# Keeping the split output weights in DRAM, moving the norm's squares to ScalarE, and a longer tile ring

## The chip, the cores and the metric

The kernel runs on one core of one Trainium2 chip, in one launch. The number that counts is the device time of that launch in microseconds (us). A core has five engines that run their own instruction streams: TensorE (PE, matrix products), VectorE (DVE), ScalarE (ACT), GpSimd (POOL) and SyncE (SP). They meet through semaphores. Data moves between DRAM and the on-chip SBUF by DMA; here SP starts nearly all DMAs and ACT a few. Products are accumulated in the eight banks of PSUM.

## The reference

Two layers on a sequence of 1024 tokens of 1024 channels. Layer 0 mixes tokens with RWKV-7, layer 1 with sparse attention (DSA). A convolutional gated FFN stands behind each. After each of the four blocks the residual is normalised:

```python
for i in range(DEPTH):
    if i % N_MIXERS == 0:
        h, v_first = rwkv7_time_mix(x, ...)      # ends with  return y @ w_o
    else:
        h = dsa_attention(x, ...)                # ends with  return o @ w_o
    x = layer_norm(DN_ALPHA * x + h, ln_g[i, 0], ln_b[i, 0])
    f = conv_ffn(x, ffn_w_up[i], ...)
    x = layer_norm(DN_ALPHA * x + f, ln_g[i, 1], ln_b[i, 1])
```

Everything is float32. The change touches `y @ w_o` and `o @ w_o` (each 1024x1024 times 1024x1024), the normalisation behind them, and the buffers of the RWKV block.

## The kernel before, in words

**Phases.** By the trace, RWKV runs to about 900 us with its output projection at 803 to 988 us, FFN 0 from about 1000 to 1740 us, DSA from 1740 to 2391 us with its output projection at 2157 to 2204 us (first half) and 2324 to 2391 us (second half), FFN 1 from about 2405 us to the end. Each block works on two halves of 512 tokens, so there are a first and a second half of each output projection.

**Split products.** A float32 product is made as three passes in a faster format. Each operand is split into `hi` (a cast, on ACT, line 54) and `lo = raw - hi` (on DVE or POOL, line 60); `mm3` (lines 65 to 67) then multiplies hi·hi, hi·lo and lo·hi. `wsplit` loads a 128x512 piece of a weight from DRAM by SP (line 124) into `wr` and splits it into `wh` and `wl`. Which engine makes `lo` stands in the table `CFG` ('p' POOL, 'v' DVE).

**Output projection.** `out_proj` handles the first half: for both column halves `ch` and eight row blocks `kt` it splits one weight piece and multiplies it with four token tiles; 16 pieces in all. `out_proj_last` handles the second half in stages. Its first stage uses pieces (kt 0 to 3, ch 0) and splits a set of "late" pieces ahead into storage that has come free (8 of them in RWKV, 12 in DSA); the next stage uses (kt 0 to 3, ch 1); its last four stages go token tile by token tile over the late pieces, add the residual and normalise. It loads and splits the weights again: 20 pieces in RWKV, where four are made twice, and 16 in DSA.

**Norm.** `residual` adds ALPHA times the input (line 143, DVE). `layer_norm_rows` takes mean and variance either by `bn_stats` and `bn_aggr` on DVE (lines 91 to 95), which the output projections use, or from sums that were collected before and two squares on ACT (lines 97 to 102), which the FFNs use already. Behind both come a power on POOL (`lnrs`, line 103), a small DVE step (`lnnm`, line 104), then the scaling (lines 106 to 111) on DVE, ACT and POOL.

**Rings.** In RWKV all 128x512 column tiles (`wh`, `wl`, `xmh`, `xml`, `xr`, `xm`) come from one ring of `k.NU` = 13 buffers, handed out in order; raw weights have their own ring `raw` of 3. In DSA's first half `wr`, `wl` and `wh` come in turn from a ring of six. A tile can be filled only when the last reader of the one that had its buffer is done. RWKV writes split pairs that it needs again to DRAM (`kept_w`, `kept_xm`) and reads them back later. The low-rank stage (`lora1`, `la` products, and `l2` products behind it) uses the four PSUM banks of `acc`.

**Order.** A scheduler lays the instructions of each engine into one fixed order ahead of time, by the order of the code and a priority; at run time each engine takes its stream in order, and a waiting instruction holds all behind it. That goes for SP's DMA queue as well.

Of the kernel before, what the change touches and what calls it, by code (L numbers as in the profile page):

```python
# [7 lines left out]
F32 = mybir.dt.float32  # L8
F32R = mybir.dt.float32r
BF16 = mybir.dt.bfloat16  # L10
AF = mybir.ActivationFunctionType
ALU = mybir.AluOpType
# [6 lines left out]
ALPHA = 4.0 ** 0.25  # L19
# [26 lines left out]
def f32(ap):  # L46
    return ap.bitcast(F32)


def split(k, raw, hi, lo, hi_eng="a", lo_eng="p"):  # L50

    nc = k.nc
    if hi_eng == "a":
        nc.scalar.copy(hi, raw)  # L54
    elif hi_eng == "v":
        nc.vector.tensor_copy(hi, raw)
    else:
        nc.gpsimd.tensor_scalar(hi, raw, 1.0, 0.0, ALU.mult, ALU.add)
    eng = nc.vector if lo_eng == "v" else nc.gpsimd
    eng.tensor_tensor(lo, raw, f32(hi), ALU.subtract)  # L60


def mm3(k, ps, lhs, rhs, start, stop, **kw):
    mm = k.nc.tensor.matmul
    mm(ps, lhs[0], rhs[0], start=start, stop=False, **kw)  # L65
    mm(ps, lhs[0], rhs[1], start=False, stop=False, **kw)  # L66
    mm(ps, lhs[1], rhs[0], start=False, stop=stop, **kw)  # L67
# [52 lines left out]
def wsplit(k, u, ap, n=512, lo_eng="v", raw=None):  # L120

    raw = (raw or u)("wr")[:, :n]
    lo, hi = u("wl", F32R)[:, :n], u("wh", F32R)[:, :n]
    k.nc.sync.dma_start(raw, ap)
    split(k, raw, hi, lo, "a", lo_eng)
    return hi, lo
# [10 lines left out]
    return Z  # L137


def residual(k, r, src, row, ch, ps):  # L140

    k.nc.sync.dma_start(r, src[row : row + 128, ch * 512 : (ch + 1) * 512])
    k.nc.vector.scalar_tensor_tensor(r, r, ALPHA, ps, ALU.mult, ALU.add)


def norm_store(k, pool, r, lnw, dst, row, eng="pp", **kw):
    layer_norm_rows(k, pool, r, *lnw, r, eng, **kw)
    for ch in range(2):
        k.nc.sync.dma_start(dst[row : row + 128, ch * 512 : (ch + 1) * 512], r[ch])


def out_proj(k, pool, u, raw, acc, res_tile, Z, w_ap, src, dst, hf, lnw):


    res = {}
    for ch in range(2):
        a = [acc("wo") for _ in range(4)]
        for kt in range(KT):
            w = wsplit(k, u, w_ap[kt * 128 : (kt + 1) * 128, ch * 512 : (ch + 1) * 512], lo_eng=CFG[("d" if raw is None else "") + "wo0"][kt], raw=raw)
            for tt in range(4):  # L160
                Zk = Z[kt // 4][:, :, kt % 4, tt * 128 : tt * 128 + 128]
                mm3(k, a[tt], (Zk[:, 0], Zk[:, 1]), w, kt == 0, kt == KT - 1)
            yield
        for tt in range(4):
            if ch == 0:
                res[tt] = res_tile()
            residual(k, res[tt][ch], src, (hf * 4 + tt) * 128, ch, a[tt])
    yield
    lnw = lnw()
    for tt in range(4):  # L170
        norm_store(k, pool, res[tt], lnw, dst, (hf * 4 + tt) * 128, CFG["ln1" if raw is None else "ln0"])
        yield


def out_proj_last(k, pool, u, raw, acc, acc1, wlate, nlate, res_tile, Z, w_ap, src, dst, hf, lnw):


    a = {}

    def w_of(kt, ch, u, lo_eng):  # L180
        return wsplit(k, u, w_ap[kt * 128 : (kt + 1) * 128, ch * 512 : (ch + 1) * 512], lo_eng=lo_eng, raw=raw)

    def part(tt, ch, kt, w):
        Zk = Z[kt // 4][:, :, kt % 4, tt * 128 : tt * 128 + 128]
        mm3(k, a[tt, ch], (Zk[:, 0], Zk[:, 1]), w, kt == 0, kt == KT - 1)

    late, order = {}, [(kt, 1) for kt in range(4)] + [(kt, ch) for ch in range(2) for kt in range(4, KT)]
    order = order[12 - nlate :]
    for tt in range(4):
        a[tt, 0] = acc("wo")  # L190
    for kt in range(4):
        w = w_of(kt, 0, u, CFG[("d" if raw is None else "") + "wl"][kt])
        for tt in range(4):
            part(tt, 0, kt, w)
        for kc in order[nlate // 4 * kt : nlate // 4 * (kt + 1)]:
            late[kc] = w_of(*kc, wlate, CFG[("d" if raw is None else "") + "wl2"])
    yield
    for pair in ((0, 1), (2, 3)):
        for tt in pair:
            a[tt, 1] = acc1("wo")  # L200
        for kt in range(4):
            w = late[kt, 1] if nlate == 12 else w_of(kt, 1, u, CFG[("d" if raw is None else "") + "wl3"][kt % 2])
            for tt in pair:
                part(tt, 1, kt, w)
        yield
    lnw = lnw()
    for tt in range(4):
        r = res_tile()
        for ch in range(2):
            for kt in range(4, KT):  # L210
                part(tt, ch, kt, late[kt, ch])
            residual(k, r[ch], src, (hf * 4 + tt) * 128, ch, a[tt, ch])
        norm_store(k, pool, r, lnw, dst, (hf * 4 + tt) * 128, CFG["ln3" if raw is None else "ln2"][2 * tt : 2 * tt + 2])
        yield


# [90 lines left out]
def rwkv(k, src, dst):  # L307
    nc, tc = k.nc, k.tc
# [8 lines left out]
    def u(name, dt=F32):  # L317
        return P_.tile([128, 512], dt, name=name, tag="u", bufs=k.NU)

    def t(name, dt=F32):  # L320
        return M_.tile([128, 512], dt, name=name, tag="t", bufs=5)
# [4 lines left out]
    def acc(name):  # L326
        return PS.tile([128, 512], F32, name=name, tag="acc", bufs=4)
# [70 lines left out]
    def raw(name):  # L398
        return P_.tile([128, 512], F32, name=name, tag="raw", bufs=3)

    def lora1(hf):
        xT = st[hf]["xT"]
        a = [acc("la") for _ in range(4)]
        for kt in range(KT):
            xx = t("xx")
            nc.vector.tensor_tensor(xx, xT[:, kt, 0:512], xT[:, kt, 1:513], ALU.subtract)
            w = raw("wl1")[:, :288]
            nc.sync.dma_start(w, k.w_l1[kt * 128 : (kt + 1) * 128, :])
            xm = {}
            for n in (3, 4, 5):  # L410
                xm[n] = u("xm")
                c = V_MIX + 8 * n + kt
                nc.vector.scalar_tensor_tensor(
                    xm[n], xx, k.vec[:, c : c + 1], xT[:, kt, 1:513], ALU.mult, ALU.add
                )

            for b, n, c0, c1, p0 in ((0, 3, 0, 64, 0), (1, 4, 64, 128, 64), (2, 5, 128, 256, 0), (3, 5, 256, 288, 96)):
                nc.tensor.matmul(
                    a[b][p0 : p0 + c1 - c0], w[:, c0:c1], xm[n], start=kt == 0, stop=kt == KT - 1
                )  # L420
        h = M_.tile([128, 512], F32, name="h", tag="h", bufs=1)
        nc.scalar.activation(h[:64], a[0][:64], AF.Tanh)
        nc.scalar.copy(h[64:], a[1][64:])
        tg = t("tg")
        nc.scalar.activation(tg, a[2], AF.Sigmoid)
        nc.sync.dma_start(gsc[hf, 0:128], tg)
        tg2 = t("tg2")
        nc.scalar.activation(tg2[96:], a[3][96:], AF.Sigmoid)
        nc.sync.dma_start(gsc[hf, 128:160], tg2[96:])
        st[hf].update(h=h)  # L430
# [66 lines left out]
    def lora2(hf, g):  # L497

        h_ = st[hf]
        AR = P_.tile([128, 4, 1024], F32, name="AR", tag="AR", bufs=2)  # L500
        BK = P_.tile([128, 4, 1024], F32, name="BK", tag="BK", bufs=1)
        s = un[hf, g] = dict(AR=AR, BK=BK)
        for i in range(4):
            p = 4 * g + i
            for o, q, v0 in ((v2(BK[:, i, :512]), slice(0, 64), V_W0), (slot(AR[:, i], 0), slice(64, 128), V_A0)):
                ps = acc("l2")
                nc.tensor.matmul(ps, wa2[q, 128 * p : 128 * p + 128], h_["h"][q], start=True, stop=True)
                s["last"] = nc.scalar.activation(o, v2(ps), AF.Sigmoid, bias=k.vec[:, v0 + p : v0 + p + 1])

# [352 lines left out]
    for j in range(-1, 5):  # L862
        for o in order:
            n, i = o[0], j + int(o[1:])
# [1025 lines left out]
def setup(tc, args, es):  # L1890
    k = Ctx()
    k.tc, k.nc = tc, tc.nc
    for n, a in zip(_INS, args):
        setattr(k, n, a)
    k.NU = 13
    k.psum = k.rows = None
    k.dram = es.enter_context(tc.tile_pool(name="scratch", bufs=1, space=bass.MemoryType.DRAM))
    C = es.enter_context(tc.tile_pool(name="consts", bufs=1, reuse_waits="tile"))
    k.ident = C.tile([128, 128], F32, name="ident")
    k.nc.sync.dma_start(k.ident, k.c_ident)  # L1900
    k.vec = C.tile([128, V_END], F32, name="vec")
    k.nc.sync.dma_start(k.vec, k.vecs)
    k.mhalf = C.tile([128, 16], F32, name="mhalf")
    k.nc.gpsimd.memset(k.mhalf, -0.5)
    return k
# [41 lines left out]
```

## Time and profile before

| | |
|---|---|
| three runs | 3111.86, 3121.84, 3131.08 us (median 3121.84) |
| profiled execution | 3114.82 us, span of its records 3113.0 us |
| PE / PE weight load | busy 2847.3 us (91%) / 2241.3 us (72%) |
| DVE | busy 2167.5 us (70%) |
| ACT | busy 1355.6 us (44%) |
| POOL | busy 1397.3 us (45%) |
| mean granted TensorE clock | 0.95 of full speed |
| DMA | 377.96 MB, 121 GB/s over the span |

The profiled execution lies 7 us under the median of the three runs and within their spread of 19 us. A duration read from it is used as it stands; a sum of differences is made against 3114.82 us and carried over to the median by adding it. Busy shares are means over phases with different limits.

### The profile page before, as it was taken

What the parts mean: (1) busy time and instruction counts of PE and PEld (TensorE: products, weight loads), DVE (VectorE), ACT (ScalarE), POOL (GpSimd) and SP (SyncE); (2) the same over time, 40 slices, a digit from 0 to 9 for tenths busy, and PEclk for the clock granted to TensorE, in tenths of its full rate; (3) what the DMA queues carried; (4) which work ended last, traced back from release to release, by engine and by line L of the source; (5) the groups of instructions that cost most, each with busy time, mean ns of one, the idle gap of its engine ahead of it and who ended that gap; (6) DMA issues with size and microseconds to landing.
All of it is one profiled execution on the core that took longest, in us unless ns stands there. A gap on an engine that the chain in (4) does not pass through costs nothing. (4 is left out here: it accounts for less than half of the span.)

```text
span 3113.0 us, 41835 instructions
## 1 busy us (share of the span) xinstructions
PE 2847.3 (91%) x15260; PEld 2241.3 (72%) x15260; DVE 2167.5 (70%) x3617; ACT 1355.6 (44%) x2332; POOL 1397.3 (45%) x939
## 2 busy tenths in 40 slices
PE   7789798999888899999999888889898899999997
PEld 3577666787666677777888665566676677777886
DVE  5777766766666888886242699995675888886142
ACT  3534234332223444444342587784363544444430
POOL 3615125131145676666462222112213766666862
PEclk9889888989898999999999889999999999999999
DMA  6745335435236122235543321113215133333740
GB/s 205 254 148 193 132 113 181 160 106 188 93 116 197 53 77 77 79 95 184 198 172 127 113 90 35 38 35 119 82 52 164 45 81 82 81 95 122 278 168 27
DMA packets 247664, 377.96 MB, mean 121 GB/s; under 512 B 18490, under 2 KB 112058, under 8 KB 247074
## 3 DMA queue, kind: packets, MB, share of 16 engines
q1 hardware_dynamic: 233634, 350.12, 34.4%
q10 hardware_dynamic: 13824, 25.17, 2.2%
q8 instruction: 120, 1.97, 0.3%
q14 instruction: 86, 0.70, 0.1%
HBM read 272.06 MB, written 103.15 MB: 121 GB/s over the span
## 5 line engine op out<-in xcount | busy, mean ns | idle before, releaser
L60 POOL TENSOR_TENSOR wo<-wr,wo 128x512 fp32r<-128x512 f32 x220 | 410.6, 1891 | 290.6 <-ACT wo L54 290.6
L1045 DVE SCALAR_TENSOR_TENSOR cv<-u,vec,cv 128x1023 f32<-128x1023 f32 (+1 forms) x176 | 342.3, 1962 | 57.9 <-ACT cv L1040 56.3
L60 POOL TENSOR_TENSOR wd<-dr,wd 128x1024 fp32r<-128x1024 f32 x88 | 226.5, 2601 | 133.1 <-ACT wd L54 133.0
L67 PE MATMUL dn<-wd,hl 128*128 128x512 f32 x704 | 274.0, 389 | 0.0
L65 PE MATMUL dn<-wd,hh 128*128 128x512 f32 x640 | 249.0, 389 | 0.0
L66 PE MATMUL dn<-wd,hh 128*128 128x512 f32 x640 | 249.0, 389 | 0.0
L65 PE MATMUL p<-xT,wo 128*128 128x512 f32 x528 | 212.1, 402 | 29.9 <-ACT u L1029 19.2
L1040 ACT ACTIVATE cv<-u,vec 128x1024 f32<-128x1024 f32 x88 | 109.5, 1244 | 243.0 <-DVE u L1034 242.9
L66 PE MATMUL p<-xT,wo 128*128 128x512 f32 x528 | 207.6, 393 | 3.0 <-DVE xT L60 3.0
L67 PE MATMUL p<-xT,wo 128*128 128x512 f32 x528 | 207.5, 393 | 2.0 <-POOL wo L60 2.0
L1642 POOL TENSOR_TENSOR cm<-sc,toep 128x256 f32<-128x256 f32 x96 | 75.8, 796 | 295.1 <-DVE mn L1658 227.7
L60 POOL TENSOR_TENSOR wo<-S,wo 128x512 fp32r<-128x512 f32 x88 | 172.5, 1978 | 30.9 <-ACT wo L54 26.6
L60 DVE TENSOR_TENSOR hl<-hr,hh 128x1024 fp32r<-128x1024 f32 x36 | 59.1, 1642 | 159.8 <-ACT hh L54 98.9
L60 POOL TENSOR_TENSOR wl<-wr,wh 128x512 fp32r<-128x512 f32 x56 | 77.4, 1382 | 184.1 <-ACT wh L54 118.7
L67 PEld LDWEIGHTS dn<-wd,hl 128*128 128x128 f32 x704 | 132.2, 188 | 27.4
L65 PEld LDWEIGHTS p<-xT,wo 128*128 128x128 f32 x528 | 99.9, 189 | 68.3 <-ACT u L1029 34.4
L65 PE MATMUL p<-x,wo 128*128 128x512 f32 x352 | 139.3, 396 | 1.3 <-DVE x L60 0.8
L54 ACT CAST wo<-wr 128x512 fp32r<-128x512 f32 x220 | 127.2, 618 | 27.8 <-POOL wo L60 17.7
L66 PE MATMUL p<-x,wo 128*128 128x512 f32 x352 | 138.9, 395 | 0.0
L54 ACT CAST wd<-dr 128x1024 fp32r<-128x1024 f32 x88 | 89.4, 1049 | 113.4 <-DMA dr<-in_w_down_dram 48.1
L67 PE MATMUL p<-x,wo 128*128 128x512 f32 x352 | 138.6, 394 | 0.0
L66 PEld LDWEIGHTS dn<-wd,hh 128*128 128x128 f32 x640 | 120.1, 188 | 25.1
(402 smaller groups left out, 8087.6 us busy)
## 6 DMA issues: line engine op xcount, KB each, us to landing
wr<-in_w_up_dram SPq DMA_DIRECT2D x88, 512.0 KB, 5.9
dr<-in_w_down_dram SPq DMA_DIRECT2D x88, 512.0 KB, 3.6
hd<-cv SPq DMA_DIRECT2D x44, 512.0 KB, 3.3
hr<-hd SPq DMA_DIRECT2D x44, 512.0 KB, 4.7
wr<-in_w_wo_dram SPq DMA_DIRECT2D x68, 256.0 KB, 3.0
wr<-in_w_rkv_dram SPq DMA_DIRECT2D x48, 256.0 KB, 4.4
kept_w<-wh ACTq DMA_DIRECT2D x48, 256.0 KB, 3.2
kept_w<-wl SPq DMA_DIRECT2D x48, 256.0 KB, 3.0
```

The source lines that it names most:

```text
L54: nc.scalar.copy(hi, raw)
L60: eng.tensor_tensor(lo, raw, f32(hi), ALU.subtract)
L65: mm(ps, lhs[0], rhs[0], start=start, stop=False, **kw)
L66: mm(ps, lhs[0], rhs[1], start=False, stop=False, **kw)
L67: mm(ps, lhs[1], rhs[0], start=False, stop=stop, **kw)
L1040: nc.scalar.activation(o, u, AF.Identity, bias=k.vec[:, cb : cb + 1], scale=k.vec[:, cw[2] : cw[2] + 1])
L1045: nc.vector.scalar_tensor_tensor(o[:, d:], u[:, : 1024 - d], k.vec[:, cw[j] : cw[j] + 1], o[:, d:], ALU.mult, ALU.add)
L1642: (nc.vector if CFG["cm"][h4] == "v" else nc.gpsimd).tensor_tensor(cm[:, :near], mk, toep[g][:, h % 8, 256 - near :], ALU.add)
```

## The change

Four edits are made together.

1. `out_proj` writes each split piece to DRAM (`kept_wo`: `wh` by ACT's queue, `wl` by SP's), and `out_proj_last` reads the pairs back by SP (line 188 of the changed kernel) instead of loading and splitting the weights again.
2. `residual` also collects row sums, and both output projections pass them to `layer_norm_rows`, so its mean comes from the sums and its variance from two squares on ACT.
3. `k.NU` goes from 13 to 19. Room for it comes from a smaller scratch area for DMA descriptors.
4. `lora1` of the first half takes the PSUM banks `mi`, `ud` and two of `st` instead of `acc`; the `l2` products of the first unit take `mi` and `ud` in turn.

```diff
-def residual(k, r, src, row, ch, ps):
+def residual(k, r, src, row, ch, ps, sums):
-    k.nc.vector.scalar_tensor_tensor(r, r, ALPHA, ps, ALU.mult, ALU.add)
+    k.nc.vector.scalar_tensor_tensor(r, r, ALPHA, ps, ALU.mult, ALU.add, accum_out=sums[:, ch : ch + 1])
...
@@ out_proj
             w = wsplit(k, u, w_ap[kt * 128 : (kt + 1) * 128, ch * 512 : (ch + 1) * 512], lo_eng=..., raw=raw)
+            d = k.kept[kt, ch] = k.dram.tile([2, 128, 512], F32, name=f"kept_wo{kt}_{ch}")
+            for j, x in enumerate(w):
+                (k.nc.scalar, k.nc.sync)[j].dma_start(d[j], f32(x))
...
+                sums[tt] = pool.tile([128, 2], F32, name="lns", tag="lns", bufs=4)
...
-        norm_store(k, pool, res[tt], lnw, dst, (hf * 4 + tt) * 128, CFG["ln1" if raw is None else "ln0"])
+        norm_store(k, pool, res[tt], lnw, dst, (hf * 4 + tt) * 128, CFG["ln1" if raw is None else "ln0"], sums=sums[tt], junk=pool.tile([128, 512], BF16, name="lnj", tag="lnj", bufs=1))
...
@@ out_proj_last
-    def w_of(kt, ch, u, lo_eng):
-        return wsplit(k, u, w_ap[kt * 128 : (kt + 1) * 128, ch * 512 : (ch + 1) * 512], lo_eng=lo_eng, raw=raw)
+    def w_of(kt, ch, u):
+        w = u("wh", F32R), u("wl", F32R)
+        for j, x in enumerate(w):
+            k.nc.sync.dma_start(f32(x), k.kept[kt, ch][j])
+        return w
...
@@ lora1
-        a = [acc("la") for _ in range(4)]
+        a = [f("la") for f in ((mi, ud, stp, stp) if hf == 0 else [acc] * 4)]
...
-                ps = acc("l2")
+                ps = ((mi, ud)[i % 2] if (hf, g) == (0, 0) else acc)("l2")
...
-    k.NU = 13
+    k.NU = 19
...
-    nc = _bacc.Bacc("TRN2", target_bir_lowering=False, num_devices=1)
+    nc = _bacc.Bacc("TRN2", target_bir_lowering=False, num_devices=1, dynamic_dma_scratch_size=1024)
```

How the streams change is seen at three places. The first is SP's queue at the turn from the first to the second half of RWKV's output projection. `wr` is a raw weight piece, `zs` a store of RWKV's result that the second half needs, `res` a residual load. Before:

```order
L124 DMA wr_7684<-in_w_wo_dram 128x512
L776 DMA zs_6_111<-v_6447 128x512
L124 DMA wr_7702<-in_w_wo_dram 128x512
L124 DMA wr_7720<-in_w_wo_dram 128x512
L124 DMA wr_7772<-in_w_wo_dram 128x512
L776 DMA zs_7_112<-v_6449 128x512
L124 DMA wr_7790<-in_w_wo_dram 128x512
L975 DMA wr_8003<-in_w_up_dram 128x8x128
L124 DMA wr_7795<-in_w_wo_dram 128x512
L142 DMA res_7575<-in_x_dram 128x512
```

Now:

```order
L188 DMA wl_7843<-kept_wo6_0_7562 128x512
L142 DMA res_7609<-in_x_dram 128x512
L142 DMA res_7614<-in_x_dram 128x512
L188 DMA wl_7843<-kept_wo6_0_7562 128x512
L788 DMA zs_7_112<-v_6449 128x512
L188 DMA wh_7827<-kept_wo0_0_7436 128x512
L188 DMA wl_7828<-kept_wo0_0_7436 128x512
L188 DMA wl_7843<-kept_wo7_0_7583 128x512
L188 DMA wh_7848<-kept_wo1_0_7457 128x512
L188 DMA wl_7849<-kept_wo1_0_7457 128x512
```

Each raw load has become two reads of a kept pair, late pieces are read ahead of the first piece, and the first piece (`kept_wo0_0`) is read right behind the last store `zs_7`.

The second is DVE in the norm of the last token tile of RWKV (`lnmv` mean and variance, `lnm` mean, `lno` its scaled negative). Before:

```order
L143 SCALAR_TENSOR_TENSOR xr_8354<-xr_8354,wo_8160 128x512
L108 SCALAR_TENSOR_TENSOR xr_8307<-xr_8307,lnrs_8337,row3_8211 128x512
L92 BN_STATS lnst_8386<-xr_8354 128x6
L93 BN_AGGR lnmv_8387<-lnst_8386 128x2
L95 TENSOR_SCALAR lnve_8383<-lnmv_8387 128x1
L106 SCALAR_TENSOR_TENSOR xr_8354<-xr_8354,lnmv_8387,row2_8209 128x512
L104 SCALAR_TENSOR_TENSOR lnnm_8385<-lnmv_8387,lnrs_8384 128x1
L108 SCALAR_TENSOR_TENSOR xr_8354<-xr_8354,lnrs_8384,row3_8211 128x512
```

Now:

```order
L143 SCALAR_TENSOR_TENSOR xr_8390,lns_8391<-xr_8390,wo_8192 128x512
L98 TENSOR_SCALAR lnm_8424<-lns_8391 128x1
L106 SCALAR_TENSOR_TENSOR xr_8339<-xr_8339,lnm_8373,row2_8233 128x512
L99 TENSOR_SCALAR lno_8425<-lnm_8424 128x1
L102 TENSOR_SCALAR lnve_8370<-lnv_8375 128x1
L104 SCALAR_TENSOR_TENSOR lnnm_8372<-lnm_8373,lnrs_8371 128x1
L108 SCALAR_TENSOR_TENSOR xr_8339<-xr_8339,lnrs_8371,row3_8235 128x512
L106 SCALAR_TENSOR_TENSOR xr_8390<-xr_8390,lnm_8424,row2_8233 128x512
L102 TENSOR_SCALAR lnve_8421<-lnv_8426 128x1
```

The statistics and their aggregate have left DVE; `lnve` of a tile now needs `lnv`, which ACT's two squares fill.

The third is ACT in the first half of DSA's output projection (`ph` belongs to the attention that runs beside it). Before:

```order
L54 CAST wh_18340<-wr_18338 128x512
L54 CAST ph_18800<-tp_18795 128x512
L54 CAST wh_18358<-wr_18356 128x512
L54 CAST wh_18376<-wr_18374 128x512
L54 CAST ph_18812<-tp_18807 128x512
L54 CAST wh_18394<-wr_18392 128x512
```

Now:

```order
L54 CAST wh_18380<-wr_18378 128x512
L54 CAST ph_18895<-tp_18890 128x512
L163 DMA kept_wo0_0_18384<-wh_18380 128x512
L54 CAST wh_18401<-wr_18399 128x512
L163 DMA kept_wo1_0_18405<-wh_18401 128x512
L54 CAST wh_18422<-wr_18420 128x512
L163 DMA kept_wo2_0_18426<-wh_18422 128x512
```

Each cast of a piece is now followed by the issue of its write, and the buffer of `wh` stays taken until that write has landed.

## Rows read from the trace of the kernel before

**Rows 1.** The first part of the profile's page: busy us of each engine, share of the span, instructions.

```profile
PE 2847.3 (91%) x15260; PEld 2241.3 (72%) x15260; DVE 2167.5 (70%) x3617; ACT 1355.6 (44%) x2332; POOL 1397.3 (45%) x939
```

**Rows 2.** Busy time of each engine by stage: length of the stretch, busy us of PE, weight load, DVE, ACT and POOL (instruction counts in brackets), granted clock, DMA share, GB/s.

```profile
300.00:400.00 100.00, 79.45 (x650) 66.24 (x649) 80.18 (x132) 24.98 (x43) 17.99 (x13) 0.83 0.40 135
...
1000.00:1740.00 740.00, 716.81 (x3171) 586.95 (x3170) 482.21 (x480) 320.21 (x489) 445.75 (x237) 0.99 0.39 124
```

**Rows 3.** The same view of the second half of RWKV's output projection, in stretches of 40 us.

```profile
880.00:920.00 40.00, 35.66 (x232) 28.37 (x232) 25.58 (x44) 10.18 (x18) 17.54 (x14) 0.94 0.38 126
920.00:960.00 40.00, 32.46 (x119) 22.69 (x117) 31.80 (x47) 17.52 (x29) 19.08 (x14) 0.85 0.73 237
```

**Rows 4.** What PE waited for from 850 to 1000 us: engine, tile and line of the waiting instruction, what released it, us in total, times, longest.

```profile
PE wo L65 <- ACT wh L54: 5.2, 3, 2.9
PE wo L66 <- POOL wl L60: 2.8, 2, 1.5
...
PE gp L66 <- DVE wl L60: 1.6, 1, 1.6
...
PE wo L66 <- DVE wl L60: 1.1, 2, 0.7
```

**Rows 5.** The same view of SP's DMA queue in that stretch, and of ACT from 895 to 960 us.

```profile
SPq L124 <- POOL wl L60: 23.7, 6, 8.1
SPq L776 <- POOL v L774: 16.4, 4, 5.8
SPq L124 <- DVE wl L60: 13.9, 10, 2.4
...
ACT wl L54 <- DMA wr<-in_w_wo_dram: 15.3, 5, 5.6
ACT wh L54 <- DMA wr<-in_w_wo_dram: 10.2, 4, 4.8
```

**Rows 6.** The DMAs from 895 to 960 us by kind: number, KB of each, median us from issue to landing.

```profile
wr<-in_w_wo_dram SPq DMA_DIRECT2D x21, 256.0 KB, 3.6
...
zt<-zs SPq DMA_DIRECT2D x4, 256.0 KB, 5.3
```

**Rows 7.** What PE waited for from 100 to 480 us, and SP in the same stretch (L442 reads kept tiles back into the ring of column tiles; L408 loads the low-rank weights into the ring `raw`).

```profile
PE xps L672 <- DVE TX L658: 20.1, 3, 16.1
...
PE pa L66 <- DMA xml<-kept_xm: 3.1, 1, 3.1
...
PE pa L65 <- DMA xmh<-kept_xm: 1.5, 1, 1.5
...
SPq L442 <- PE pa L67: 83.0, 17, 16.4
SPq L408 <- PE la L418: 63.1, 5, 52.6
```

**Rows 8.** Busy time by engine in the stretch of the second low-rank stage, as in rows 2.

```profile
365.00:405.00 40.00, 23.73 (x317) 22.07 (x317) 36.81 (x64) 5.20 (x9) 0.00 (x0) 0.55 0.00 1
```

**Rows 9.** What PE waited for from 44 to 110 us.

```profile
PE pa L65 <- ACT xmh L54: 13.1, 3, 11.3
```

**Rows 10.** Durations of the two ways to the statistics. The first two lines are groups of 895 to 1000 us (busy us, mean ns of one); the next two are the squares in FFN 0 with the read of their sum, the last the read of the row sum behind FFN's residual (ns: shortest, median, longest).

```profile
L92 DVE BATCH_NORM_STATS2 lnst<-xr 128x6 f32<-128x512 f32 x8 | 5.4, 681 | 0.0
...
L93 DVE BATCH_NORM_AGGREGATE lnmv<-lnst 128x2 f32<-128x12 f32 x8 | 1.5, 201 | 0.0
...
L101 ACT ACTIVATE lnj<-acc,lno x16: 705/722/732, 1563.6 to 1727.9; 128x512 bf16<-128x512 f32 x16
L101 ACT ACTIVATION_READ_ACCUMULATOR lnj<-acc,lno x16: 185/187/199, 1564.2 to 1728.6; 128x1 f32 x16
...
L1173 DVE DVE_READ_ACCUMULATOR acc<-acc,dn x32: 76/83/85, 1552.1 to 3099.3; 128x1 f32 x32
```

**Rows 11.** The last two norms of RWKV in order of time: start, duration, engine, line, tile; in brackets the idle time before it and who ended it.

```profile
988.60 0.99 POOL L103 TENSOR_TENSOR lnrs<-lnve,mhalf 128x1 f32<-128x1 f32 x1
...
991.93 0.15 DVE L95 TENSOR_SCALAR lnve<-lnmv 128x1 f32<-128x1 f32 x1
...
992.25 1.61 POOL L111 TENSOR_TENSOR xr<-xr,row 128x512 f32<-128x512 f32 x1
993.83 0.54 POOL L103 TENSOR_TENSOR lnrs<-lnve,mhalf 128x1 f32<-128x1 f32 x1
```

**Rows 12.** The first half of DSA's output projection, 2157 to 2204 us: a group of POOL, the longest named wait of PE and that of ACT.

```profile
L60 POOL TENSOR_TENSOR wl<-wr,wh 128x512 fp32r<-128x512 f32 x16 | 20.6, 1290 | 37.6 <-ACT wh L54 37.6
...
PE wo L65 <- ACT wh L54: 0.8, 1, 0.8
...
ACT wh L54 <- PE wo L66: 18.0, 8, 3.0
```

**Rows 13.** The writes of kept pairs that RWKV makes already, from the page's list of DMA issues (as in rows 6).

```profile
kept_w<-wh ACTq DMA_DIRECT2D x48, 256.0 KB, 3.2
kept_w<-wl SPq DMA_DIRECT2D x48, 256.0 KB, 3.0
```

**Rows 14.** What PE waited for from 2204 to 2405 us.

```profile
PE pt L938 <- DVE xr L143: 2.9, 1, 2.9
PE lg L65 <- DVE mn L1658: 2.7, 2, 1.5
...
PE ol L66 <- DVE pl L60: 1.9, 5, 0.9
```

More of the change, by code (lines that the diff above doesn't have):

```diff
@@ L155, in out_proj @@
     res = {}
+    k.kept, sums = {}, {}
     for ch in range(2):
@@ L166, in out_proj @@
                 res[tt] = res_tile()
-            residual(k, res[tt][ch], src, (hf * 4 + tt) * 128, ch, a[tt])
+                sums[tt] = pool.tile([128, 2], F32, name="lns", tag="lns", bufs=4)
+            residual(k, res[tt][ch], src, (hf * 4 + tt) * 128, ch, a[tt], sums[tt])
     yield
@@ L191, in out_proj_last @@
     for kt in range(4):
-        w = w_of(kt, 0, u, CFG[("d" if raw is None else "") + "wl"][kt])
+        w = w_of(kt, 0, u)
         for tt in range(4):
@@ L195, in out_proj_last @@
         for kc in order[nlate // 4 * kt : nlate // 4 * (kt + 1)]:
-            late[kc] = w_of(*kc, wlate, CFG[("d" if raw is None else "") + "wl2"])
+            late[kc] = w_of(*kc, wlate)
     yield
@@ L201, in out_proj_last @@
         for kt in range(4):
-            w = late[kt, 1] if nlate == 12 else w_of(kt, 1, u, CFG[("d" if raw is None else "") + "wl3"][kt % 2])
+            w = late[kt, 1] if nlate == 12 else w_of(kt, 1, u)
             for tt in pair:
@@ L208, in out_proj_last @@
         r = res_tile()
+        sums = pool.tile([128, 2], F32, name="lns", tag="lns", bufs=4)
         for ch in range(2):
@@ L211, in out_proj_last @@
                 part(tt, ch, kt, late[kt, ch])
-            residual(k, r[ch], src, (hf * 4 + tt) * 128, ch, a[tt, ch])
-        norm_store(k, pool, r, lnw, dst, (hf * 4 + tt) * 128, CFG["ln3" if raw is None else "ln2"][2 * tt : 2 * tt + 2])
+            residual(k, r[ch], src, (hf * 4 + tt) * 128, ch, a[tt, ch], sums)
+        norm_store(
+            k, pool, r, lnw, dst, (hf * 4 + tt) * 128, CFG["ln3" if raw is None else "ln2"][2 * tt : 2 * tt + 2],
+            sums=sums, junk=pool.tile([128, 512], BF16, name="lnj", tag="lnj", bufs=1),
+        )
         yield
```

## The prediction

> **What bounds the kernel now.** I read the page's busy shares first, then the busy time by stage, then the waits of PE and of the DMA queue in the stages that the change touches, then single durations. PE is busy for 91% of the span [rows 1]; the others lie far under it. So time can come back only from PE's gaps and from stretches in which its granted clock is the lower of its two levels (1.2 instead of 2.4 GHz, 0.5 in the rows). The FFNs have next to none of either (716.81 of 740 us busy at 0.99 [rows 2]) and the change leaves their order alone. The edits meet four places: RWKV's units, the second half of RWKV's output projection, DSA's output projection, and the norm tails behind both second halves. None removes work of PE, so each is worth at most the gaps and the low clock at its own place.
>
> **The second half of RWKV's output projection** is the place with most to win. Its ceiling: from 880 to 920 us PE is idle for 40 - 35.66 = 4.3 us and runs at 0.94; from 920 to 960 us it is idle for 7.5 us at 0.85 [rows 3]. Priced as busy time times the missing clock, that is 0.06 x 35.66 = 2.1 and 0.15 x 32.46 = 4.9 us. Idle and clock give 18.9 us. What PE waits for by name is the split: 5.2 us for the cast `wh`, 2.8 and 1.1 us for `wl`, 1.6 us for `wl` of the gate weights, which stay [rows 4]. Behind the casts stands the chain: ACT waits 15.3 + 10.2 us for raw pieces to land, and SP cannot issue these since 23.7 + 13.9 us of its time go to waiting for splits that free `raw` buffers [rows 5]. The change cuts this chain: no cast, no subtraction, no ring of 3; a pair needs two reads. I take away all three waits on `wh` and `wl` of `wo`, 9.1 us, and some clock with them.
>
> Against it stand three things. First, bytes: 20 pairs are read as 40 tiles of 256 KB where 20 raw pieces were, 5 MB more, where the DMA share is already 0.73 at 237 GB/s [rows 3]. Scaled to a share of 1 that is some 325 GB/s (an estimate from that row), so 5 MB are 16 us more of a busy DMA. Second, SP's order: the reads of the first pair now stand behind the last `zs` store, and SP waits for POOL's `v` before such stores, 16.4 us in four [rows 5]; in the old order raw pieces stand there just the same. Third, stores of the first half's norm, paced by POOL at about 5 us a tile (from one `lnrs` to the next, 988.60 to 993.83 [rows 11]), still stand ahead of pairs for the next stage. Between a full 18.9 us and nothing I take 10 us, near the named waits of 9.1. What is late next is the landing of pairs: 256 KB land in 3.6 us here, in 5.3 where four are issued together [rows 6]. Bounds: -19 to +4 us, the latter if the pairs land later than the splits were ready.
>
> What hides the writes of the first half: 16 pieces in some 108 us of PE work (803 to 911 us), with a DMA share of 0.38 even at the end [rows 3]. I cost them at nothing; without that cover the price is that of DSA's first half, next.
>
> **DSA's output projection, first half.** 16 pieces stand here in 47 us, and the longest named wait of PE for one is 0.8 us [rows 12]: nothing to win. The change adds two writes per piece. Per piece, 47 / 16 = 2.9 us, the traffic goes from 256 to 768 KB, some 270 GB/s, against the 325 GB/s estimated above. The buffers come from a ring of six, two pieces, so a `wh` or `wl` is wanted again two pieces later, and now needs its write landed besides the last product on it. ACT waits 18.0 us for `PE wo` before casts [rows 12]: PE still frees a buffer last. A write lands in 3.0 to 3.2 us in RWKV [rows 13]. For `wl` there are 2 x 2.9 us from one fill of a buffer to the next, less POOL's 1.29 us for the fill [rows 12] and some 0.4 us in SP's queue: 4.2 us, so about 1 us of slack; for `wh` it is more. Below that nothing happens; beyond, each piece is late by the excess. I take +2 us, bounds 0 and +16 (1 us for each of 16).
>
> The Trainium skill says in "DMA: Bandwidth & Descriptors", section "Issuing engines are not separate DMA queues", that transfers started by ScalarE and SyncE run on the same 16 DMA engines and interleave, and that two issuers save only the time of starting them. By it the split of the writes between ACT and SP would relieve nothing here, and with the upper end of +16 in place of +2 the sum below would be +2 instead of -12 us. The trace of before has no stretch with writes on both queues beside dense reads in a ring of six, so no row decides.
>
> **DSA's second half and the attention beside it.** Over both blocks 34 subtractions and 32 statistics leave DVE, and 36 casts leave ACT for 32 squares. PE waits for DVE here only in short pieces: 2.9 for the residual, 2.7 for `mn`, 1.9 for `pl` [rows 14]. I take -2 us of these 7.5. The first piece's products now stand in a row ahead of attention's, with pairs that wait for buffers: bounds -5 to +5.
>
> **The norm tails.** Statistics of a tile's last half took 0.681 + 0.201 us plus `lnve` 0.15, together 1.03. Now: the row sum 0.083, `lnm` and `lno` at 0.15 each (taken from `lnve`, like them 128x1), two squares with their sums at 0.722 + 0.187, `lnve` 0.15: 2.35 us [rows 10, 11]. That is 1.3 us later per tile. In the last tile `lnve` ends at 992.08 and POOL starts `lnrs` at 993.83, since it is at line 111 until then [rows 11]: 1.75 us of slack cover it as long as POOL is the pace. Two hops between engines eat part of it. +0.5 us for each of two tails, +1 in all; bounds 0 and +3 if the cover is gone.
>
> **The ring of 19.** SP waits 83.0 us for products to free ring buffers from 100 to 480 us [rows 7], which looks large. But PE waits for such loads only 3.1 + 1.5 us; its largest wait, 20.1 us, is for DVE's triangular inverse `TX`, where DVE is busy for 36.81 of 40 us with no DMA at all [rows 8]. A longer ring cannot shorten that. SP's other wait, 63.1 us for `la` [rows 7], is on the ring of raw weights, which stays at 3. I take -3 of the 4.6 us; bounds -10 (clock that returns with it, since PE runs at 0.83 from 300 to 400 us [rows 2]) to +5 (splits done earlier on DVE delay the inverse).
>
> **The low-rank stage.** Its banks free `acc` for the first projection, which however starts on `xmh` from ACT (13.1 us of waiting [rows 9]). ACT's evacuations are the same in number. 0, bounds -1 and +1; what hides the gain is that wait.
>
> **Sum.** -10 + 2 - 2 + 1 - 3 + 0 = -12 us. Against the profiled 3114.82 us that is 3102.8; against the median 3121.84 it is 3109.8, so I forecast 3110 us.
>
> **The rivals.** *More than the gaps.* All of the 18.9 us, the 10 of the ring, and 5 of DSA: -34 us, 3088 us. It needs the pairs to be there before PE asks and the clock to stay at its upper level through 920 to 960 us. For it speaks that the low clock there comes with short waits: 0.85 stands beside 7.5 us of gaps of which none by name is longer than 2.9 us [rows 3, 4]. Against it: the bytes. The Trainium skill's page "TensorE: Matmul & The Clock Gate", section "HAM oscillation — how this bites in real kernels", tells of kernels in which waits for DMA between groups of products throw the engine back to the lower clock, so that a wait costs more than its length. By that the gain would be nearer 18.9 than 9.1 us at this place; rows 3 agree that idle and low clock stand together, but don't tell which leads.
>
> *The waits only change their names.* The reads stand in the same queue behind the same `zs` and `x` stores, and PE waits for DMA where it waited for ACT; the ring's loads are hidden already. Then -10 and -3 fall away: +1 us, 3123 us. The fixed order of PE and SP speaks for it.
>
> *Slower: the writes hold the ring of DSA's first half.* If two writes and a read per piece take landings from 3.0 us to the 5.3 us that four transfers at once show [rows 6], the slack of 1 us is gone and each of 16 pieces is late by about 1.3 us: +21 us; the same crowding takes the gain of RWKV's second half: 3121.84 + 21 + 1 - 2 - 3 = 3139 us. It decides from a landing of about 4.2 us on. To be slower by over 1% the pairs of RWKV's second half must come late as well, by about 16 us more of DMA time.
>
> That the change does nothing can be left out: casts and subtractions are gone from the streams.
>
> **How the numbers follow.** Forecast 0.45, more than the gaps 0.2, other names 0.2, slower 0.15. A measurement of this kernel can tell about 1% from no change, 31 us. Of the second case (3088 us and below) some eight tenths lie past that, and a little of the forecast's lower end: faster 0.2. Of the last case a third: slower 0.05. The rest, 0.75, is within 1%. For the range I add the bounds of the forecast's own terms as far as they are likely together (-25 to +10 around -12) and reach to the middle of the neighbours: 3080 to 3135 us.
>
> **What the profile after would show.** Right: the waits `wo <- ACT wh` and `wo <- wl` gone from 900 to 960 us, the stretch from the second half's first product to FFN 0 shorter by about 10 us at a clock above 0.85; `TX` still 16 us; in DSA's first half PE without gaps over 1 us and kept writes landing under 4.2 us; `lnrs` of the last tile still released by POOL's own work. Wrong: PE waiting for `kept_wo` reads in RWKV's second half for as long as for splits before; SP or ACT waiting for landed writes in DSA's first half; or a large change from 100 to 480 us, where I count on next to none.

## The result, and the profile after

| | before | after |
|---|---|---|
| median | 3121.51 us (6 runs, 3111.86 to 3131.08) | 3096.23 us (6 runs, 3086.51 to 3101.03) |
| profiled execution, span | 3114.82, 3113.0 us | 3088.9, 3087.1 us |
| ratio | | 0.9917, 95% interval 0.9899 to 0.9935 |

The change gains 0.83% or 26 us (20 to 32). The forecast was 12 us, with the same sign and 3096 us inside its range of 3080 to 3135. The size is what needs explaining: which edit brought twice the sum.

The first view of the kernel after is the busy time by stage, in the columns of [rows 2], for RWKV's units (100 to 770 us) and for its output projection. The lines of the kernel before for the same stretches are in the second fence.

```profile
100.00:770.00 670.00, 617.48 (x4650) 482.58 (x4650) 492.43 (x756) 242.16 (x404) 221.66 (x182) 0.90 0.50 169
770.00:1000.00 230.00, 202.53 (x1442) 160.44 (x1442) 143.21 (x271) 77.25 (x145) 90.42 (x74) 0.91 0.56 190
```

```profile
100.00:770.00 670.00, 609.73 (x4606) 474.31 (x4604) 480.28 (x732) 235.31 (x394) 216.47 (x180) 0.89 0.49 164
770.00:1000.00 230.00, 201.47 (x1413) 158.12 (x1414) 155.45 (x268) 65.68 (x112) 83.01 (x67) 0.89 0.39 129
```

PE's idle time in the units fell from 60.3 to 52.5 us. In the second stretch the output projection ends earlier, so that 27 us of FFN 0 lie in it as well. By the starts of PE's products, the last product of the units' projections (`pa`) stands 9.4 us earlier, the first product of FFN 0 26.2 us earlier (972.8 instead of 998.9 us), and the last product of the kernel 25.7 us. So in these two executions the units gave about 9 us and the output projection about 17; DSA and the FFNs gave nothing.

What PE waited for after in the units (the view of [rows 7], here from 100 to 770 us), and before in the same stretch:

```profile
PE xps L684 <- DVE TX L670: 25.6, 3, 14.9
PE pa L65 <- ACT xmh L54: 7.0, 3, 5.2
...
PE pa L67 <- DMA wl<-kept_w: 0.6, 2, 0.5
```

```profile
PE xps L672 <- DVE TX L658: 24.6, 4, 16.1
...
PE pa L66 <- DMA xml<-kept_xm: 3.1, 1, 3.1
...
PE pa L65 <- DMA xmh<-kept_xm: 1.5, 1, 1.5
PE pa L67 <- DMA wl<-kept_w: 1.3, 2, 1.1
...
PE pa L67 <- DMA xml<-kept_xm: 0.5, 2, 0.3
...
PE pa L65 <- DMA wh<-kept_w: 0.3, 1, 0.3
```

The waits for kept tiles, 6.7 us in all, are down to 0.6; the one for `TX` hardly moved (24.6 and 25.6 us in all). In the output projection (the view of [rows 4], 885 to 985 us after) no product of `wo` waits for a cast or a subtraction of its weights any more; one gap of 6.4 us stands before the gate products:

```profile
PE gp L65 <- DVE zt L819: 6.4, 1, 6.4
PE pt L950 <- POOL xr L111: 3.8, 2, 2.0
```

The stretches after, in the columns of [rows 3], show where that gap lies, and the DMA beside it:

```profile
890.00:910.00 20.00, 19.23 (x85) 15.51 (x83) 11.19 (x30) 8.17 (x19) 7.95 (x7) 1.00 0.86 295
910.00:930.00 20.00, 13.96 (x62) 10.82 (x63) 7.82 (x14) 6.40 (x12) 8.39 (x7) 0.83 1.00 353
930.00:950.00 20.00, 19.04 (x96) 15.77 (x95) 5.20 (x9) 3.32 (x7) 8.55 (x7) 1.00 0.73 271
```

`gp` waits for a multiplication by `zt`, and that for the load of `zt`. SP's queue has the four loads (line 815) behind stores of the first half's norm (line 149), before one of which SP waited 3.1 us for POOL, and behind three reads of late pieces (line 188):

```profile
900.70 3.84 SPq L149 DMA_DIRECT2D x<-res  x2
904.60 1.39 SPq L188 DMA_DIRECT2D wl<-kept_wo  x3
906.09 1.80 SPq L815 DMA_DIRECT2D zt<-zs  x4
```

A `zt` load takes 5.4 us to land (median), and from 910 to 930 us the DMA engines are full at 353 GB/s.

### The profile page after: what moved, and what is told of

Same layout as the page of the kernel before. It is cut to its first block, busy times and chain, and to the rows that moved or that the text cites. A ratio compares the mean times of both kernels' runs of the same rounds, so it can differ in the third digit from the quotient of the medians.

```text
span 3087.1 us, 41906 instructions
## 1 busy us (share of the span) xinstructions
PE 2845.2 (92%) x15260; PEld 2244.2 (73%) x15260; DVE 2124.7 (69%) x3599; ACT 1359.8 (44%) x2360; POOL 1391.9 (45%) x937
## 5 line engine op out<-in xcount | busy, mean ns | idle before, releaser
L65 PE MATMUL p<-xT,wo 128*128 128x512 f32 x528 | 213.4, 404 | 25.1 <-ACT u L1041 18.9
L66 PEld LDWEIGHTS dn<-wd,hh 128*128 128x128 f32 x640 | 120.2, 188 | 25.1
L65 PEld LDWEIGHTS dn<-wd,hh 128*128 128x128 f32 x640 | 120.2, 188 | 24.8
```

## Which edit does it

A single execution of the same instructions can lie 10 us off in the units (see the last section), so the verdicts go by the medians, and by waits and idle times within a trace, not by where a stretch starts. "Measured" gives the ratio to the kernel before on the same chip with its 95% interval, and the difference in us of 3120. By the traces the 13.3, 28.7 and 26.6 us that two expectations name as the changed kernel's lead are 12.9, 28.3 and 26.2; nothing rests on the difference. The code of each edit is shown in part; `...` marks what is left out.

### The four edits alone

Ring of 19 with the scratch that makes room for it; kept weights; low-rank banks; norm:

```diff
-    k.NU = 13
+    k.NU = 19
...
```

> The ring of 19 alone (with the smaller descriptor scratch that makes room), all else as before. The changed kernel's trace has the first product of RWKV's output projection 13.3 us earlier than before, where the prediction gave the ring 3 us. Theory A, the ring: about -10 to -13 us against the kernel before, with SP's waits for ring buffers from 100 to 480 us down from 83 to about 27 us and the output projection starting 10 us or more earlier. Rival, the prediction's own size: -3 us (0 to -5); then the rest comes from the low-rank banks or from the order that only all edits together give.

Measured: 0.9939 (0.9918 to 0.9960), -19 us (-26 to -12). The ring alone brings most of the gain: theory A, and more than its 10 to 13 us. The prediction's 3 us for it were wrong. The smaller scratch area isn't the cause: the norm alone, below, has it too and gives 0. SP's waits for ring buffers fell as expected, from 83.0 [rows 7] to 25.1 us; in its one trace the output projection starts 6.4 us earlier, not 10 or more. That trace shows no wait for kept tiles over 0.3 us in the units:

```profile
PE pa L67 <- DMA wl<-kept_w: 0.3, 1, 0.3
PE pa L66 <- DMA wl<-kept_w: 0.2, 1, 0.2
```

It also shows, with the weights still split a second time, waits of `wo` from 885 to 985 us of 1.3 us for `wh` and 0.3 for `wl` where 9.1 stood before [rows 4]:

```profile
PE wo L65 <- ACT wh L54: 1.3, 1, 1.3
...
PE wo L66 <- DVE wl L60: 0.3, 1, 0.3
```

```diff
...
-        return wsplit(k, u, w_ap[...], lo_eng=lo_eng, raw=raw)
...
+        for j, x in enumerate(w):
+            k.nc.sync.dma_start(f32(x), k.kept[kt, ch][j])
...
```

> The kept output weights alone, ring of 13 and statistics as before. Theory A: the second half of RWKV's output projection gains about 13 to 15 us and DSA nothing, -13 us in all; casts and subtractions no longer stand before PE there, and a DMA share near 1 leaves one gap of some 6 us. Prediction's own size: -10 + 2 = -8 us. Rival, that the gain there needs the longer ring or the freed DVE: -5 us or less.

Measured: 1.0007 (0.9991 to 1.0023), nothing: the rival, the gain needs more than this edit. The trace shows PE's waits under a new name, 885 to 985 us, and in SP's queue the two reads that they are for:

```profile
PE wo L65 <- DMA wh<-kept_wo: 9.9, 2, 6.2
```

```profile
903.38 0.32 SPq L187 DMA_DIRECT2D wh<-kept_wo  x1
...
910.19 4.07 SPq L149 DMA_DIRECT2D x<-res  x2
914.36 0.37 SPq L187 DMA_DIRECT2D wh<-kept_wo  x1
```

9.9 us for pairs instead of 9.1 for splits. PE's gaps end at 908.8 and 917.1 us. The first read stands behind reads of late pieces and residual rows that SP issued from 898 us on without waiting for a buffer. The second stands right behind a store of the first half's norm, for which SP had waited 3.3 us for POOL. So both are late by their place in SP's fixed order; SP's waits for PE in that stretch (5.8 and 5.0 us) lie elsewhere.

```diff
-        a = [acc("la") for _ in range(4)]
+        a = [f("la") for f in ((mi, ud, stp, stp) if hf == 0 else [acc] * 4)]
...
```

> The low-rank banks alone. The prediction: 0 (-1 to +1). Rival A: +2 us, since the second low-rank products take two banks in turn instead of four and PE waits for ACT's evacuations. Rival B: -3 us or more, since the first projection finds its accumulators free; that would be a part of the 13.3 us ahead of the output projection.

Measured: 1.0001 (0.9988 to 1.0015): 0, as predicted, from -4 to +5 us. That leaves room for rival A's +2 and just for rival B's -3.

```diff
-    k.nc.vector.scalar_tensor_tensor(r, r, ALPHA, ps, ALU.mult, ALU.add)
+    k.nc.vector.scalar_tensor_tensor(r, r, ALPHA, ps, ALU.mult, ALU.add, accum_out=sums[:, ch : ch + 1])
...
```

> The norm from row sums and squares alone (with the smaller descriptor scratch for its tiles). The prediction: +1 us from two tails, -2 us from DVE in DSA. Theory A: the tail from the last output product to FFN 0's first product is 2 us longer than before (the changed kernel's trace: 28.7 us ahead at the last product, 26.6 at FFN 0), 0 to +3 us in all. Rival: -3 us or more, since statistics that leave DVE free the splits of the second half.

Measured: 1.0002 (0.9981 to 1.0022): nothing that can be told from 0 (-6 to +7 us), so neither theory A nor the rival is decided. The tail from the last product of `wo` to FFN 0 is 12.0 us, 10.8 before.

### One edit taken back

```diff
...
-            k.nc.sync.dma_start(f32(x), k.kept[kt, ch][j])
...
+        return wsplit(k, u, w_ap[...], lo_eng=lo_eng, raw=raw)
...
```

> The changed kernel without the kept output weights (ring of 19, new norm and low-rank banks stay). So far the ring alone gave -19 us, the kept weights alone nothing. Theory A, the ring is the gain and frees the same waits that the kept weights were to free: about -17 us, 6 to 9 us slower than the changed kernel. Rival, that the kept weights pay nothing even with the ring: -25 us, like the changed kernel. Rival, that they pay their predicted 10 us only with the ring: -15 us or less gain.

Measured: 0.9943 (0.9928 to 0.9958), -18 us. Theory A: against the -26 of the changed kernel the kept weights are worth some 8 us on top of the ring. By the two intervals that difference is 1 to 15 us, so its sign is just clear of the noise and its size is not.

```diff
-    k.NU = 19
+    k.NU = 13
```

> The changed kernel with the ring back at 13. Theory A: the whole gain hangs on the ring, 0 us (-4 to +4) against the kernel before. Rival: the edits other than the ring pay 8 us by themselves, -8 us.

Measured: 0.9967 (0.9954 to 0.9980), -10 us: the rival. With the ring of 13, kept weights, norm and banks together gain what none of them gains alone. Which of them need each other isn't settled, and the trace doesn't show where the 10 us come from: it has 4.1 us of waits for pairs instead of the 9.9 above, but 5.5 us for a residual row:

```profile
PE wo L65 <- DVE res L143: 5.5, 1, 5.5
PE wo L65 <- DMA wh<-kept_wo: 4.1, 1, 4.1
```

Ring and kept weights alone, without the other two:

```diff
...
+            d = k.kept[kt, ch] = k.dram.tile([2, 128, 512], F32, name=f"kept_wo{kt}_{ch}")
...
-    k.NU = 13
+    k.NU = 19
...
```

> Ring of 19 and kept weights, without the new norm and the low-rank banks. Theory A: all of the change's gain, -25 us, since norm and low-rank banks alone gave 0. Rival: about -19 us, the ring's own, and the rest comes from norm or banks once the waits in front of them are gone.

Measured: 0.9926 (0.9906 to 0.9946), -23 us. Nearer to theory A; the intervals don't part it from -19.

The traces, one execution each, point the same way as the 8 us. From the last `pa` product of the units to FFN 0's first product it is 233 us before, 225 and 235 us with the ring of 19 but weights split again (ring alone, kept weights taken back), 228 and 225 us with kept weights and a ring of 13 (kept weights alone, ring taken back), and 216 us in the two so far with the ring of 19 and kept weights.

### Where the ring pays

```diff
+    def uo(name, dt=F32):
+        return P_.tile([128, 512], dt, name=name, tag="uo", bufs=6)
...
-                return out_proj(k, P_, u, raw, acc, res, Z, k.w_wo, src, dst, hf, lnw)
+                return out_proj(k, P_, uo, raw, acc, res, Z, k.w_wo, src, dst, hf, lnw)
...
```

`out_proj_last` takes `uo` in the same way.

> The kernel before with a ring of its own of 6 tiles for the split weights of RWKV's output projection; all other column tiles, the residual rows too, keep the ring of 13. If the ring's gain lies in the output projection (the first half's residual rows hold 8 of the 13 tiles there): -8 to -17 us with the waits of wo for the splits nearly gone from 900 to 960 us. If it lies in the units ahead of it, where the prediction looked: 0 to -4 us.

Measured: 0.9978 (0.9966 to 0.9990), -7 us (-11 to -3). The output projection has a part of the gain, a little below the range named for it, and the interval reaches into both ranges. The waits of `wo` for `wh` are down to 2.6 us, none is left for `wl`, and one of 2.7 us for a residual row is new.

```diff
+    hold = [u("hold") for _ in range(6)]
+    for h in hold:
+        nc.vector.memset(h[:, :1], 0.0)
     z0, finish0 = post(0)
...
     run(last)
+    for h in hold:
+        nc.vector.tensor_tensor(h[:, 1:2], h[:, :1], k.fin[:, :1], ALU.add)
...
-    k.NU = 13
+    k.NU = 19
...
```

> The ring of 19 alone, but with 6 of its tiles written and held from the end of RWKV's units to the last product of its output projection (released by six tiny DVE reads there, about 1 us on the tail), so that the units have 19 and the output projection 13. Theory A, two separate gains: the units' part, -8 to -11 us, with PE idle for about 52 us from 100 to 770 us and the waits of wo for splits back between 900 and 960 us; with the -7 us of the ring of 6 for the output projection alone it makes up the -19 of the ring. Rival, that the output projection takes nearly all of it: 0 to -4 us.

Measured: 0.9975 (0.9960 to 0.9991), -8 us, theory A. The units have their gain, and the output projection has its old waits back. First the stretch of the units as above, then the waits of `wo` from 885 to 990 us:

```profile
100.00:770.00 670.00, 619.35 (x4633) 483.49 (x4631) 483.29 (x749) 234.78 (x392) 219.40 (x181) 0.89 0.48 165
```

```profile
PE wo L65 <- ACT wh L54: 3.9, 4, 2.8
PE wo L66 <- DVE wl L60: 2.8, 2, 2.0
PE wo L66 <- POOL wl L60: 2.3, 2, 1.8
```

PE is idle for 50.7 us in the units, like all kernels with 19 (50 to 53 us; those with 13 have 57 to 61). The three waits are 9.0 us, as in [rows 4]. -8 for the units and -7 for the output projection make up -15 of the ring's -19; those two are uncertain by 4 to 5 us each, so the rest is within the intervals.

```diff
-    k.NU = 19
+    k.NU = 16
```

> The changed kernel with a ring of 16. Theory A, loads come early enough once the ring holds some tiles more: -18 us (about halfway between the -10 of 13 and the -26 of 19), with waits of pa for kept tiles from 100 to 770 us at 2 us or less (6 to 10 with 13, none with 19). Rival, that the last three tiles bring nothing: -25 us.

Measured: 0.9968 (0.9952 to 0.9983), -10 us, like the same kernel with 13. Neither theory A nor the rival: 16 is no halfway house. The waits for kept tiles in the units are all there:

```profile
PE pa L66 <- DMA xml<-kept_xm: 4.6, 2, 4.1
PE pa L67 <- DMA wl<-kept_w: 2.4, 3, 1.2
PE pa L65 <- DMA xmh<-kept_xm: 1.3, 1, 1.3
```

The step lies between 16 and 19; why it lies there was not tried and stays open.

The changed kernel with the ring divided into 13 and 6:

```diff
...
-    k.NU = 19
+    k.NU = 13
...
-                return out_proj(k, P_, u, raw, acc, res, Z, k.w_wo, src, dst, hf, lnw)
+                return out_proj(k, P_, uo, raw, acc, res, Z, k.w_wo, src, dst, hf, lnw)
...
```

> The changed kernel with the ring of 19 divided: 13 for RWKV's units and all other column tiles, 6 of their own for the weight pieces and pairs of the output projection. Theory A, the kept weights need free buffers in the output projection and the units need the longer ring by themselves: the stretch from the last unit's projection to FFN 0 shortens by about 14 us as in the changed kernel, while PE's idle time from 100 to 770 us stays near 60 us as in all kernels with 13 (52 with 19); -15 to -18 us in all. Rival, that both need the one ring of 19: -10 us, like the other three edits with a ring of 13.

Measured: 0.9977 (0.9967 to 0.9986), -7 us (-10 to -4): the rival's number. PE's idle time in the units stays at 57.3 us, as theory A had it, but the stretch from the units to FFN 0 shortens by 7 us (226 instead of 233) and not by 14. Six buffers of their own do end the waits for pairs (0.7 us left), but the gate products then wait for the cast of their own weights:

```profile
PE gp L65 <- ACT wh L54: 6.2, 1, 6.2
```

In ACT's order that cast stands right behind a scaling of the first half's norm, which had waited 3.0 us for DVE. So theory A had the waits for pairs right and the gain wrong: something else was late next. Whether the gate weights were ordered so late for want of ring buffers isn't shown.

### The gap that is left

```diff
-'rt': 'f2 l0 z f0 f1 p0 p2 l1 ...'
+'rt': 'f2 z l0 f0 f1 p0 p2 l1 ...'
```

> The changed kernel with the second half's last gate products and transposes (z in the table that orders the output projection's steps) taken ahead of the first stage of pairs, so that the four zt loads stand ahead of most pair reads in SP's queue. The changed kernel shows one gap of 6.4 us there, gp waiting for zt at a DMA share of 1.00. Theory A, the order of the queue makes that gap: -4 to -6 us against the changed kernel, -30 us against the kernel before. Rival, the bytes make it (the DMA engines are full from 910 to 930 us): the wait moves to wo for a late pair, 0 us against the changed kernel, -26 us.

Measured: 0.9911 (0.9890 to 0.9932), 3096.37 us; the changed kernel had 0.9917 and 3096.23 us. The gap of `gp` is gone, and PE waits 1.6 and 0.9 us for late pairs instead; from 930 to 950 us the DMA engines are full:

```profile
910.00:930.00 20.00, 17.24 (x73) 12.96 (x72) 12.75 (x29) 11.19 (x24) 12.03 (x11) 0.91 0.84 282
930.00:950.00 20.00, 19.42 (x93) 15.66 (x92) 2.58 (x4) 3.29 (x6) 8.89 (x7) 1.00 1.06 385
```

PE is busy for 36.7 instead of 33.0 us of these 40 us, but the median doesn't show it. Theory A named the cause of the gap rightly, SP's order, but the rival has the time: -28 us against the kernel before, no gain to be told over the changed kernel. A gain of some us isn't excluded, none is shown.

## Why the prediction was right or wrong

**The ring of 19** is the step that failed: -3 us forecast with bounds of -10 and +5, -19 alone. Two things went wrong in it. The stretch read was 100 to 480 us, with 4.6 us of waits for kept tiles; to 770 us they are 6.7, and with the longer ring nearly all go and PE's idle time falls by 8 us. And the ring was priced only in the units. The output projection takes its tiles from the same ring, where by the code the residual rows of the first half (two tiles for each of four token tiles, the listing's `res`) hold 8 of the 13.

SP's 23.7 + 13.9 us of waits for splits [rows 5] were read as the chain that makes the pieces late, by the ring `raw` of 3. With the ring of 19 alone and `raw` untouched these waits are not shorter (28.5 + 20.5 us from 850 to 1000 us), and yet PE's 9.1 us for casts and subtractions fall to 1.6; holding six tiles brings them back to 9.0. What differs is ACT's order. Before, the cast at 914.25 us is the one that the second half's first product waits for; it stands behind late pieces (`wl`) and two casts of FFN 0's weights (here `wo`):

```profile
912.69 0.62 ACT L54 CAST wl<-wr 128x512 fp32r<-128x512 f32 x1 [2.07 <-DMA wr<-in_w_wo_dram]
913.21 1.13 ACT L54 CAST wo<-wr 128x512 fp32r<-128x512 f32 x2
914.25 0.61 ACT L54 CAST wh<-wr 128x512 fp32r<-128x512 f32 x1
```

With the ring of 19 alone, casts of weight pieces follow directly on the late piece, at 907.09 and 907.94 us, FFN 0's come after 914 us, and that product waits 1.1 us for a residual row instead:

```profile
906.56 0.62 ACT L54 CAST wl<-wr 128x512 fp32r<-128x512 f32 x1 [5.66 <-DMA wr<-in_w_wo_dram]
907.09 0.61 ACT L54 CAST wh<-wr 128x512 fp32r<-128x512 f32 x1
```

With six tiles held the order is again that of before. So in this stage the ring acts at least in part through the order that is fixed ahead of time; ACT's waits at run time for products to free a tile fall as well, from 6.7 to 1.8 us (870 to 960 us). That the order is what it is for want of free tiles is inferred: nothing but the ring's length and the scratch area was changed. (That six tiles can stay held while the rest of the ring goes on also shows that its buffers are not handed out strictly in order, as the section on rings has it.) The argument that `TX` would not move was right: 16.1 before, 14.9 after for the longest wait.

The forecast of 3110 us was 14 us too slow. That 3096 still lies within 3080 to 3135 us is luck as far as the mechanism goes: the term that brought most lay outside its own bounds.

**RWKV's second half**, -10 forecast; the stretch gave about -17, of which the kept weights' own share is some 8 us (from -18 to -26). The sum was near for this place, for a reason that was half right: no split is waited for any more, but with the ring of 13 that gave nothing. There the second rival, "the waits only change their names", came true word for word (9.1 us for splits, 9.9 for pairs). The three things against the gain were there: the DMA share went to 1.00, with 353 GB/s over 20 us where 325 had been estimated as the most; the reads land in 5.3 to 5.8 us, where 5.3 was named as what is late next; and a gap of 6.4 us is the price.

The kinds of DMA after, 880 to 945 us, in the columns of [rows 6]:

```profile
wl<-kept_wo SPq DMA_DIRECT2D x25, 256.0 KB, 5.3
wh<-kept_wo SPq DMA_DIRECT2D x12, 256.0 KB, 5.8
```

**DSA's first half**, +2 forecast with +16 as the bound: nothing came. The writes land faster than any landing that the forecast used, well under the 4.2 us at which they would hold the ring (2131 to 2180 us after; before, 2157 to 2206 us, DMA moved 77 GB/s at a share of 0.23):

```profile
kept_wo<-wh ACTq DMA_DIRECT2D x16, 256.0 KB, 2.6
kept_wo<-wl SPq DMA_DIRECT2D x16, 256.0 KB, 2.1
```

```profile
2131.00:2180.00 49.00, 47.74 (x210) 38.10 (x211) 6.25 (x16) 11.30 (x19) 20.65 (x16) 1.00 0.75 256
```

ACT waits for such a write once, 3.0 us, and PE not for that. The Trainium skill's page "DMA: Bandwidth & Descriptors", section "Issuing engines are not separate DMA queues", says that DMAs started by ScalarE and SyncE run on the same 16 engines. The trace agrees: SP's queue took 52.2% and ACT's 22.6% of the 16 engines' time, together the share of 0.75. The forecast's upper end did not follow from it: at 0.75 there was room. The slower rival falls with it. (Its 1.3 us a piece don't fit its own limit either: 5.3 less 4.2 us is 1.1, or 18 us and not 21.)

**DSA's second half** (-2) gave nothing either; from 1000 us to the end PE's products keep their distance from before (25.3 to 25.7 us in both FFNs; in DSA the middle of each 50 us lies between 24 and 27).

**The norm tails**: +1 forecast, +0.5 each. The one of RWKV is 12.9 us after, 10.8 before, and 12.0 with the norm alone; the one of DSA is 12.9 us after and 14.3 before. Together that is +0.7, so the sum came out by two misses of opposite sign. The cover in RWKV held as described: the last `lnve` ends at 965.79 us and POOL starts `lnrs` when its line 111 is done. The 2.1 us lie ahead of that: POOL's last `lnrs` starts 7.8 us behind the last `wo` product, before 5.6.

```profile
965.58 0.21 DVE L102 TENSOR_SCALAR lnve<-lnv 128x1 f32<-128x1 f32 x1 [0.27 <-ACT lnj L101]
...
966.51 1.26 POOL L111 TENSOR_TENSOR xr<-xr,row 128x512 f32<-128x512 f32 x1
967.73 0.55 POOL L103 TENSOR_TENSOR lnrs<-lnve,mhalf 128x1 f32<-128x1 f32 x1
```

**The low-rank stage**: 0 forecast, 0 measured (-4 to +5).

**More than the gaps** (3088 us) lies nearer the result than the forecast's centre: 3096. It came by the ring more than by the clock, which from 770 to 1000 us went from 0.89 to 0.91 only, and from 910 to 930 us still stood at 0.83 beside the 6.4 us gap. What [rows 3] left open, whether idle time or low clock leads, the changed kernel's trace shows at that gap (columns as there). PE is idle from 909.2 to 915.7 us; the clock is full until 912 us, falls from 912 to 914 us, and is 0.50 (1.2 GHz) when PE works again, until 920 us:

```profile
910.00:912.00 2.00, 0.00 (x0) 0.00 (x0) 1.40 (x3) 1.41 (x3) 1.22 (x1) 1.00 0.85 272
912.00:914.00 2.00, 0.00 (x0) 0.00 (x0) 0.00 (x0) 0.00 (x0) 1.92 (x3) 0.82 1.03 396
918.00:920.00 2.00, 2.00 (x7) 1.28 (x5) 0.98 (x2) 0.00 (x0) 0.00 (x0) 0.50 1.10 337
920.00:922.00 2.00, 1.62 (x9) 1.20 (x9) 0.96 (x3) 1.07 (x2) 0.00 (x0) 0.97 1.03 397
```

Here the idle time leads, and 4.3 us at half the clock cost some 2 us more than the gap itself (an estimate from these rows). That fits what the Trainium skill's page "TensorE: Matmul & The Clock Gate", section "HAM oscillation — how this bites in real kernels", tells of waits for DMA between products; the change's gain didn't come from it.

## What to carry to other kernels

When a ring of buffers is lengthened, price it at every stage that draws from it, and count who holds its tiles for long: here residual rows held 8 tiles of 13, the waits bore the name of splits, and six tiles for the split weights alone gave 7 us. A short ring need not show as a wait for a buffer: where the order is laid ahead of time, it can show as work that stands behind something less urgent, so compare the orders. Replacing work on other engines by a reload gave nothing while the ring was short, since the wait only got a new name, and some 8 us with the longer ring. And test edits together as well as alone: of these four, one gives 19 us, the others nothing that can be told from 0, the three without the ring 10 together, and all of them 26.

## What the runs showed of the hardware

Identical launches on one chip spread widely: 29 runs of the kernel before took 3109 to 3129 us, and their mean granted clock went with it, from 0.944 in the four at 3126 us on average to 0.950 in the two at 3112. The traces show the same: to the end of the units, kernels with the ring of 13, whose streams hardly differ there, lie from 4.7 us ahead of the kernel before to 10.0 us behind it, while PE's idle time is the same within 4 us (57.3 to 60.7 us from 100 to 770 us). Differences of 10 us in one trace are no evidence there.

Second, in the changed kernel the time from issue to landing doesn't follow the mean traffic. Writes of split pairs, 256 KB each, took 4.2 (ACT's queue) and 3.8 us (SP's) in the units at 169 GB/s and a share of 0.50 (medians, 100 to 770 us), but 2.6 and 2.1 us in DSA's first half at 256 GB/s and 0.75. Reads of pairs took 5.3 to 5.8 us in RWKV's second half, 880 to 945 us, at 316 GB/s on average. What sets the time, bursts or the mix of reads and writes, was not tried.
